# Attention ordered by pairs of heads, with sample attention in four rounds and the patterns combined in between

## Chip, cores and metric

One core of a Trainium2 chip runs the whole program. The time is the device time of one execution in microseconds (us). The engines work in parallel, each through its own queue in order, and meet at semaphores: TensorE (PE, with its weight loads PEld), VectorE (DVE), ScalarE (ACT), GpSimd (POOL) and SyncE (SP). SP and POOL issue the DMA transfers.

## The reference

One step of a decoder layer on a prompt of 2048 tokens and on 64 sample tokens (8 sequences of 8), 1024 channels wide. What matters here:

```python
proj = h @ w_in      # u, v, z of branch A; q, k, v of 3 patterns x 8 heads x 64; z of B; gates
DILATED_PAIRS = ((128, 1), (512, 4), (2048, 16))     # window, dilation
for gi, (window, dilation) in enumerate(DILATED_PAIRS):
    if kv_caches is None:   # prompt: causal band of window/dilation keys of the strided sequence
        acc, m, l = _dilated_prompt(q[:, :, gi], k[:, :, gi], v[:, :, gi], window, dilation)
    else:                   # sample: window/dilation + 1 keys out of the cache and the new rows
        acc, m, l = _dilated_sample(q[:, :, gi], k[:, :, gi], v[:, :, gi], kv_caches[gi], window, dilation)
...
wts = jnp.exp(ms - jnp.max(ms, axis=0))                    # over the three patterns, per head
attn = jnp.sum(wts[..., None] * accs, axis=0) / jnp.sum(wts * ls, axis=0)[..., None]
y_b = attn * silu(z_b)
```

So head slot j needs the results of all three patterns for slot j, and of no other slot. Branch A (gMLP gating), the merge of both branches and the output projection follow.

## The kernel before

All tensors are float32 outside; projections split each operand into two float16 halves and use three matmuls a product. The program runs in this order:

1. Conditioning and normalised inputs `hT`, with the first two projections of V mixed in.
2. The attention loop: 12 units `i` of a pattern `g` and a pair of heads `hp`, with `g, hp = divmod(i, 4)`: all four pairs of pattern 0, then of pattern 1, then of pattern 2. A unit has 8 steps. A step is `scores` (PE scores, masked minimum on DVE, exponentials on ACT, split into float16 halves `hl`, transposed by a DMA into `pT`) and, one step later, `values`. Between them, generators supply PE: `qk_proj(i + 1)` projects the next unit's queries and keys, and `extras(i)` the rest of V, the gate path `zb` and the gates. Results of a unit go to memory (`asc`).
3. `qk_proj` also transposes keys for the cache outputs (`kf` to `ko`, L746) right behind the projection's group, through the one PSUM bank `t`.
4. `sample_attention` is one generator, advanced two steps (`STEP1`) per step of the loop from unit 3 on. It computes key products of pattern 0, 1 and 2 for half the heads at a time (`ch` tiles of cache rows, product L472 and sum L473 on DVE) when `ready` says that all units of the pattern are projected, then a maximum over everything, then value products (L542, L547). Before each pattern, `repeat` copies the queries in memory 16 times (`qr`, 2 MB) and the new keys and values (`kr`); POOL issues these and all other transfers of the sample attention.
5. Branch A: projection of `v`, then gating. Between them `combine` weights the three patterns, one tile of 128 tokens and all heads at a time (16 calls), and the sample attention runs on. Its last step transposes `tot` (L573).
6. Merge and output projection.

The order that a reader sees is not the order that runs: a list scheduler places every engine's instructions by a simulated timeline, with the program's order as priority. It is fixed when the program is built.

Of the kernel before, what the change touches and what calls it, by code (L numbers as in the profile page):

```python
# [1 line left out]

# [16 lines left out]
SEQ = 2048  # L19
# [46 lines left out]
def body(ctx, tc, I, O):  # L66
# [18 lines left out]
    STEP1 = 2  # L85
# [31 lines left out]
    qr_d = [dram.tile([128, 8 * 512], F32, name=f"qr{g}") for g in range(3)]  # L117
    kr_d = [[dram.tile([NS, (8, 1)[g] * 512], F32, name=f"kr{g}{k}") for k in range(2)] for g in range(2)]
# [207 lines left out]
    def plan():  # L326
        qk = lambda i: [(o + i * 128, 128) for o in (OQ, OK)]
        order.extend((OVV + u * 256, 256) for u in range(2))
        order.extend(qk(0))
        for i in range(12):  # L330
            if i < 11:
                order.extend(qk(i + 1))
            if i < 4:
                order.append((OVV + 512 + i * 256, 256))
            elif i < 6:
                order.append((OZB + (i - 4) * 256, 256))
# [51 lines left out]
    def sample_attention(sp):  # L388
# [7 lines left out]
        tot = sp.tile([64, 2, 260], F32, name="tot")  # L396
        m_d = dram.tile([128, 64], F32, name="m_d")
        mn_d = dram.tile([64, 8], F32, name="mn_d")
        ma_d = dram.tile([64, 8], F32, name="ma_d")

        def repeat(g):
# [3 lines left out]
            for k, d in enumerate((ks_d, vs_d)):  # L405
                if g == 0:
                    GDMA(kr_d[0][k], bass.AP(tensor=d[0].tensor, offset=d[0].offset,
                                             ap=[[4096, 8], [0, 8], [1, 4096]]))
                elif g == 1:
                    GDMA(kr_d[1][k], bass.AP(tensor=d[1].tensor, offset=d[1].offset,  # L410
                                             ap=[[4096, 8], [0, 2], [1, 2048]]))
            yield

        def rows4(g, j, u, kv, hh):

            t = sp.tile([128, 4, 256], F32, tag="ch", bufs=CHB, name="ch")
            c = caches[g]
            pstep, r0 = ((8, j), (32, 4 * j), (128, 16 * j + 4 * u))[g]
            GDMA(t, bass.AP(tensor=c.tensor, offset=c.offset + r0 * 1024 + kv * 512 + hh * 256,  # L419
                            ap=[[pstep * 1024, 128], [1024, 4], [1, 256]]))  # L420
            return t

        def pairs(g, kv, hh):

            if g == 0:
                for j0 in (0, 4):
                    t = rows4(0, j0, 0, kv, hh)
                    for i in range(4):
                        for u in range(2):
                            yield t[:, i:i + 1, :].to_broadcast([128, 4, 256]), 4 * u, j0 + i, None  # L430
            elif g == 1:
                for j in range(8):
                    t = rows4(1, j, 0, kv, hh)
                    yield t, 0, j, None
                    yield t, 4, j, t
            else:
                for j in range(8):
                    for u in range(2):
                        t = rows4(2, j, u, kv, hh)
                        yield t, 4 * u, j, t  # L440

        def new_rows(g, n0, n, kv, hh):
            t = sp.tile([64, 4, 256], F32, tag="pr", bufs=1, name="nw")
            d = (ks_d, vs_d)[kv][g]
            c = slice(hh * 256, hh * 256 + 256)
            if g == 0:
                GDMA(t[:, 0:n, :], kr_d[0][kv].rearrange("p (n c) -> p n c", n=8)[:, n0:n0 + n, c])
            else:
                GDMA(t[:, 0, :], d[:, c])
                if g == 1:  # L450
                    GDMA(t[:, 1, :], kr_d[1][kv][:, c])
            return t[:, 0:n, :]

        NEW = [(0, 0, 0, 4), (0, 4, 4, 4), (1, 8, 0, 2), (2, 10, 0, 1)]

        Sx = [sp.tile([128, 8, 8, 8], F32, name=f"S{g}") for g in range(3)]
        Sn = sp.tile([64, 11, 8], F32, name="Sn")
        mp = sp.tile([128, 3, 8, 8], F32, name="mp")

        for g in range(3):  # L460
            for hh in range(2):
                cs = slice(hh * 256, hh * 256 + 256)
                h4 = slice(hh * 4, hh * 4 + 4)
                if hh == 0:
                    while ready[0] < g:
                        yield
                    yield from repeat(g)
                q = sp.tile([128, 8, 256], F32, tag="qa", bufs=1, name="q")
                GDMA(q, qr_d[g].rearrange("p (t c) -> p t c", t=8)[:, :, cs])
                for rows, t0, j, own in pairs(g, 0, hh):  # L470
                    dst = own if own is not None else sp.tile([128, 4, 256], F32, tag="pr", bufs=1, name="pr")
                    V.tensor_tensor(dst, rows, q[:, t0:t0 + 4, :], op=ALU.mult)  # L472
                    V.tensor_reduce(Sx[g][:, j, t0:t0 + 4, h4], dst.rearrange("p t (h c) -> p t h c", h=4),  # L473
                                    axis=AX.X, op=ALU.add)
                    yield
                qn = sp.tile([64, 1, 256], F32, tag="qn", bufs=1, name="qn")
                GDMA(qn[:, 0, :], qs_d[g][:, cs])
                for (gg, i0, n0, n) in NEW:
                    if gg == g:
                        k = new_rows(g, n0, n, 0, hh)  # L480
                        V.tensor_tensor(k, k, qn.to_broadcast([64, n, 256]), op=ALU.mult)
                        V.tensor_reduce(Sn[:, i0:i0 + n, h4], k.rearrange("p n (h c) -> p n h c", h=4), axis=AX.X,
                                        op=ALU.add)
                yield
            if g < 2:
                V.tensor_tensor(Sx[g], Sx[g], cms[:, g].unsqueeze(3).to_broadcast([128, 8, 8, 8]), op=ALU.add)
            V.tensor_reduce(mp[:, g], Sx[g].rearrange("p j t h -> p t h j"), axis=AX.X, op=ALU.min)
            yield
        V.tensor_tensor(Sn, Sn, mnew.unsqueeze(2).to_broadcast([64, 11, 8]), op=ALU.add)


        V.tensor_tensor(mp[:, 0], mp[:, 0], mp[:, 1], op=ALU.min)
        V.tensor_tensor(mp[:, 0], mp[:, 0], mp[:, 2], op=ALU.min)
        mn = sp.tile([64, 8], F32, name="mn")
        V.tensor_reduce(mn, Sn.rearrange("p n h -> p h n"), axis=AX.X, op=ALU.min)
        GDMA(m_d, mp[:, 0].rearrange("p t h -> p (t h)"))
        GDMA(mn_d, mn)
        mg = sp.tile([8, 17, 64], F32, tag="pr", bufs=1, name="mg")
        GDMA(mg[:, 0:16, :].rearrange("b p c -> b (p c)"), m_d.rearrange("(b p) c -> b (p c)", b=8))
        GDMA(mg[:, 16, :], mn_d.rearrange("(b t) h -> b (t h)", b=8))  # L500
        ma = sp.tile([8, 64], F32, name="ma")
        V.tensor_reduce(ma, mg.rearrange("b p c -> b c p"), axis=AX.X, op=ALU.min)
        GDMA(ma_d.rearrange("(b t) h -> b (t h)", b=8), ma)
        m64 = sp.tile([64, 8], F32, name="m64")
        GDMA(m64, ma_d)
        mb = sp.tile([128, 8, 8], F32, name="mb")
        pb = bank("t", bufs=TB)
        PE.matmul(pb[:, 0:64], selB, ma, start=True, stop=True)
        V.tensor_copy(mb, pb[:, 0:64].rearrange("p (t h) -> p t h", t=8))
        yield  # L510


        for g in range(3):
            V.tensor_tensor(Sx[g], Sx[g], mb.unsqueeze(1).to_broadcast([128, 8, 8, 8]), op=ALU.subtract)
            S.activation(Sx[g], Sx[g], AF.Exp, scale=-1.0)
            V.tensor_reduce(mp[:, g], Sx[g].rearrange("p j t h -> p t h j"), axis=AX.X, op=ALU.add)
            yield
        V.tensor_tensor(mp[:, 0], mp[:, 0], mp[:, 1], op=ALU.add)
        V.tensor_tensor(mp[:, 0], mp[:, 0], mp[:, 2], op=ALU.add)
        V.tensor_tensor(Sn, Sn, m64.unsqueeze(1).to_broadcast([64, 11, 8]), op=ALU.subtract)  # L520
        S.activation(Sn, Sn, AF.Exp, scale=-1.0)
        ln = sp.tile([64, 8], F32, name="ln")
# [719 lines left out]
```

## Time and profile before

| | |
|---|---|
| time, median of 3 runs | 2649.3 us (2641.63 to 2649.64) |
| the profiled execution | 2646.09 us; its span 2644.2 us |
| busy: PE, DVE, ACT, POOL | 2498.0, 1710.2, 981.4, 203.8 us |
| mean granted clock of PE | 0.974 |
| DMA | 392.24 MB, mean 148 GB/s; POOL's queue 73.71 MB of it |
| attention loop (first to last masked score) | 217 to 1447 us |
| branch A, then merge and output | from 1447 us; the last gating operation (L1100) starts at 2146.8 us |

How to read it: PE is busy nearly throughout, so what the other engines do matters where PE waits for them or where its granted clock falls below 1 behind a wait. A group's row gives busy time, mean duration in ns of one instruction, and idle time of its engine just before it with the releaser.

### The profile page before, as it was taken

To read this page: it belongs to the slowest core of one execution; us is meant where nothing else is said; L and a number is where in the kernel's file an instruction comes from. 1 tells how busy PE (TensorE), PEld (TensorE's weight loads), DVE (VectorE), ACT (ScalarE), POOL (GpSimd) and SP (SyncE) were. 2 spreads that over 40 slices of the span, in tenths; PEclk is the share of its full clock that TensorE was granted. 3 is DMA by queue.
4 is the path that set the end of the run, shared out by engine and by line. 5 is a ranking of instruction groups with operands and counts; after the bars stand their busy time and mean duration, and the time that the engine had idled before them with its cause. 6 is when DMAs were issued, how large, how long until landed. Compare 5 with 4: busy or idle time off the path is not lost.

```text
span 2644.2 us, 47549 instructions
## 1 busy us (share of the span) xinstructions
PE 2498.0 (94%) x18471; PEld 1777.3 (67%) x18471; DVE 1710.2 (65%) x3665; ACT 981.4 (37%) x2329; POOL 203.8 (8%) x223
## 2 busy tenths in 40 slices
PE   6999999899999899999998899999999699999998
PEld 3865776757767555555555678555555368898998
DVE  8655544888444787433478569899998535555653
ACT  7434544344555335445333222211111023443422
POOL 3000000000000010000021000100001101111110
PEclk8999999999999999999999999999999799999999
DMA  7233545556444577334577653665344237656552
GB/s 277 83 108 76 130 98 138 162 127 169 109 98 113 166 151 173 90 102 119 146 231 208 185 160 113 202 188 162 114 126 136 88 122 250 198 178 207 189 167 73
DMA packets 506673, 392.24 MB, mean 148 GB/s; under 512 B 180215, under 2 KB 443431, under 8 KB 505902
## 3 DMA queue, kind: packets, MB, share of 16 engines
q1 hardware_dynamic: 486718, 315.48, 42.6%
q0 software_dynamic: 19728, 73.71, 8.8%
q8 instruction: 145, 2.38, 0.4%
q14 instruction: 82, 0.67, 0.1%
HBM read 258.98 MB, written 99.43 MB: 136 GB/s over the span
## 4 chain that ended last, share of the span: by engine, by line
PE 51%; issue 19%; DVE 13%; DMA 12%; ACT 2%; POOL 1%; SPq 1%; DVEq 0%; POOLq 0%; ACTq 0%
PE mm L352 10%; PE mm L353 10%; PE mm L354 10%; DMA ch<-in_cache_kv_w 4%; PE mm L362 3%; PE mm L363 3%; PE mm L364 3%; PE s L828 2%; PE o L873 1%; DVE S L473 1%; DVE acc L547 1%; PE s L364 1%; PE s L362 1%; PE s L363 1%; POOL ch L419 1%
## 5 line engine op out<-in xcount | busy, mean ns | idle before, releaser
L352 PE MATMUL mm<-hH,hl 128*128 128x512 f16 (+2 forms) x2240 | 775.7, 346 | 10.2 <-DVE e L1099 4.5
L353 PE MATMUL mm<-hL,hl 128*128 128x512 f16 (+2 forms) x2240 | 774.6, 346 | 0.0
L354 PE MATMUL mm<-hH,hl 128*128 128x512 f16 (+2 forms) x2240 | 773.7, 346 | 0.0
L362 PE MATMUL mm<-hl,hH 128*128 128x256 f16 x1536 | 421.3, 276 | 7.5 <-ACT vt L625 2.8
L363 PE MATMUL mm<-hl,hL 128*128 128x256 f16 x1536 | 423.0, 276 | 0.8 <-DVE hL L617 0.7
L364 PE MATMUL mm<-hl,hH 128*128 128x256 f16 x1536 | 422.6, 276 | 0.4 <-DVE hl L308 0.4
L352 PEld LDWEIGHTS <-hl 128*128 128x128 f16 x2240 | 223.5, 100 | 185.0 <-issue 14.1
L353 PEld LDWEIGHTS <-hl 128*128 128x128 f16 x2240 | 221.6, 99 | 184.4 <-issue 17.4
L354 PEld LDWEIGHTS <-hl 128*128 128x128 f16 x2240 | 221.5, 99 | 183.9 <-issue 6.8
L838 ACT ACTIVATE p<-p,sg 128x256 f32<-128x256 f32 (+1 forms) x384 | 172.3, 451 | 177.9 <-DVE sg L836 152.4
L362 PEld LDWEIGHTS <-hH 128*128 128x128 f16 x1536 | 152.2, 99 | 30.3 <-issue 6.8
L363 PEld LDWEIGHTS <-hL 128*128 128x128 f16 x1536 | 152.0, 99 | 26.7 <-issue 6.3
L836 DVE CUSTOM_DVE_ANT_0 p<-s,masks,cqk 128x256 f32<-128x256 f32 (+1 forms) x384 | 140.5, 422 | 45.0 <-PE s L828 45.0
L296 DVE TENSOR_REDUCE mx<-wr 128x1 f32<-128x512 f32 x160 | 108.0, 681 | 93.5 <-DMA wr<-in_w_in 92.2
L364 PEld LDWEIGHTS <-hH 128*128 128x128 f16 x1536 | 152.1, 99 | 19.4 <-issue 0.7
L277 ACT ACTIVATE wh<-wr 128x512 fp32r<-128x512 f32 x160 | 99.8, 630 | 114.3 <-PE mm L353 71.0
L307 ACT ACTIVATE hl<-wr,scw 128x512 f16<-128x512 f32 x160 | 105.1, 712 | 98.1 <-DVE scw L303 95.6
L419 POOL DMA_DIRECT2D ch<-in_cache_kv_w x104 | 78.5, 755 | 816.0 <-DVE pr L542 241.5
L852 DVE SCALAR_TENSOR_TENSOR hl<-p,hl 128x1024 f16<-128x1024 f32 (+2 forms) x100 | 95.4, 954 | 69.5 <-ACT hl L851 68.6
L308 DVE SCALAR_TENSOR_TENSOR hl<-wr,scw,hl 128x512 f16<-128x512 f32 x160 | 113.4, 745 | 15.2 <-ACT hl L307 15.2
L1098 ACT ACTIVATE e<-mm,scw 128x512 f32<-128x512 f32 (+2 forms) x40 | 24.4, 611 | 250.8 <-PE mm L354 239.5
L352 PE MATMUL mm<-yaH,wh 128*128 128x512 f32 (+1 forms) x320 | 113.0, 353 | 1.9 <-DVE gts L1176 1.9
(445 smaller groups left out, 4384.5 us busy)
## 6 DMA issues: line engine op xcount, KB each, us to landing
ch<-in_cache_kv_w POOLq DMA_DIRECT2D x104, 512.0 KB, 4.6
wr<-in_w_in SPq DMA_DIRECT2D x160, 256.0 KB
wr<-in_w_proj_a SPq DMA_DIRECT2D x64, 256.0 KB
wr<-in_w_out SPq DMA_DIRECT2D x64, 256.0 KB
a<-sg SPq DMA_DIRECT2D x48, 264.0 KB
c<-a SPq DMA_DIRECT2D x48, 264.0 KB
v<-vt SPq DMA_DIRECT2D x96, 128.0 KB
vr<-v SPq DMA_DIRECT2D x48, 256.0 KB
```

The source lines that it names most:

```text
L296: V.tensor_reduce(mx[:, j:j + 1], raw.rearrange("p k c -> p (k c)"), axis=AX.X, op=ALU.max, apply_absolute_value=True)
L307: S.activation(HL[:, 0], raw, AF.Copy, scale=sc[:, 0:1])
L308: V.scalar_tensor_tensor(HL[:, 1], raw, sc[:, 0:1], HL[:, 0], op0=ALU.mult, op1=ALU.subtract)
L352: PE.matmul(pt, h, xh[:, t0:t0 + n], start=kc == 0, stop=False)
L353: PE.matmul(pt, h, xl[:, t0:t0 + n], start=False, stop=False)
L354: PE.matmul(pt, l, xh[:, t0:t0 + n], start=False, stop=kc == m - 1)
L362: PE.matmul(pt, xh[:, t0:t0 + n], h, start=kc == 0, stop=False)
L363: PE.matmul(pt, xl[:, t0:t0 + n], h, start=False, stop=False)
L364: PE.matmul(pt, xh[:, t0:t0 + n], l, start=False, stop=kc == m - 1)
L419: GDMA(t, bass.AP(tensor=c.tensor, offset=c.offset + r0 * 1024 + kv * 512 + hh * 256, ap=[[pstep * 1024, 128], [1024, 4], [1, 256]]))
L836: V.tensor_tensor_reduce(x, sb[e][:, j, 0:nk], masks[:, 256 - nk:256], scale=cqk[:, i:i + 1], scalar=3e38, op0=ALU.add, op1=ALU.min, accum ...
L838: S.activation(x, x, AF.Exp, bias=mc, scale=-1.0, accum_out=lc)
```

## The change

Units go by pair of heads: `g, hp = i % 3, i // 3`, so the three patterns of a pair follow one another. What depends on it moves with it:

- `plan`, `extras` and the first V projections follow the new order (V of heads 0 to 3 for the three patterns first, then `zb` and the second halves); `v_scale` works on one pattern and half the heads, and is called half a unit ahead of its use.
- `sample_attention` runs in four rounds, one per pair of heads, each with keys, maximum, values and output. It starts with the loop, three steps per step (`STEP1 = 3`); round `hp` may begin when unit `3 * hp + 1` is done. A `ch` tile holds 8 cache rows of 128 channels instead of 4 of 256. `repeat`, `qr_d` and `kr_d` are gone: eight transfers per pattern read the queries (and as many the new rows of patterns 0 and 1) straight into each group of partitions.
- `combine(hp, q)` takes one pair of heads and 512 tokens. Twelve of sixteen run inside the attention loop, in two parts with loads in the first; the others in the projection of `v`. None is left in the gating.
- PE's transposes of queries, keys and combined rows are put into a list, `later`; `flush(1)` runs all but the newest entry.

The core of the diff:

```diff
-    STEP1 = 2
+    STEP1 = 3
...
-            GDMA(qr_d[g], bass.AP(tensor=qs_d[g].tensor, offset=qs_d[g].offset,
-                                  ap=[[4096, 8], [0, 16], [1, 4096]]))
...
-                q = sp.tile([128, 8, 256], F32, tag="qa", bufs=1, name="q")
-                GDMA(q, qr_d[g].rearrange("p (t c) -> p t c", t=8)[:, :, cs])
...
+        for hp in range(4):
+            while ready[0] < hp:
+                yield
+            for (g, i0, n) in NEW:
+                q = sp.tile([128, 8, 128], F32, tag="qa", bufs=1, name="q")
+                for b in range(8):
+                    from_d(q[b * 16:b * 16 + 16], qs_d[g][b * 8:b * 8 + 8, :], hp, [[0, 16], [512, 8], [1, 128]])
...
+                for rows, t0, nt, j, own in pairs(g, 0, hp):
...
     def qk_proj(i):
-        g, hp = divmod(i, 4)
+        g, hp = divmod(i, 3)[::-1]
...
-                        p2 = bank("t", (128, 4, 128))
-                        for j, (a, w) in enumerate(parts):
-                            PE.transpose(p2[0:w, j, :], kf[:, a:a + w], ident)
...
+                        later.append(partial(key_rows, g, hp, t0, lo, parts, kf))
...
+    def flush(keep=0):
+        while len(later) > keep:
+            later.pop(0)()
...
-    def combine(i):
-        cc = cb.tile([128, 3, 528], F32, tag="c", bufs=1, name="c")
+    def combine(hp, q):
+        c = cb.tile([128, 3, 4, 132], F32, tag="c", bufs=1, name="c")
         for g in range(3):
-            DMA(cc[:, g, :], asc[g][i * 128:(i + 1) * 128, :])
+            DMA(c[:, g], rows_of(asc[g][:, hp * 132:(hp + 1) * 132], 0, q))
...
+        yield
...
-        pt = bank("s")
+        later.append(partial(y_rows, hp, q, zt))
...
+    sp = sx_.enter_context(tc.tile_pool(name="smp", bufs=1, side="right"))
+    smp[0] = sample_attention(sp)
     for i in range(12):
-        if i in (3, 7):
-            v_scale((i + 1) // 4)
-        if i == 3:
-            sp = sx_.enter_context(tc.tile_pool(name="smp", bufs=1, side="right"))
-            smp[0] = sample_attention(sp)
...
+        if i and i % 3 == 0:
+            todo_c = iter([x for q in range(4) for x in [combine(i // 3 - 1, q)] * 2])
         for b in range(8):
...
+            if b == 3 and i % 6 < 2:
+                v_scale(1 + i % 6, i // 6)
...
             for gen in todo[len(todo) * b // 8:len(todo) * (b + 1) // 8]:
                 next(gen)
+                flush(1)
...
             step(STEP1)
+            if i >= 3 and s % 3 == 0:
+                next(next(todo_c), None)
...
-        if i in (2, 6, 10):
-            ready[0] = (i - 2) // 4
+        if i % 3 == 1:
+            ready[0] = i // 3
```

What the scheduler makes of it, at three places. First POOL's queue at the start of the sample work (`qs`, `ks`, `vs` are the sample rows in memory, `qr`, `kr` their copies, `ch` a cache tile, `qn`, `nw` new rows). Before:

```order
L407 DMA kr_92<-vs_85 64x1x4096
L477 DMA qn<-qs_79 64x256
L410 DMA kr_94<-vs_86 16x1x2048
L403 DMA qr_88<-qs_79 128x1x4096
L469 DMA q<-qr_88 128x8x256
L407 DMA kr_91<-ks_82 64x1x4096
L419 DMA ch<-in_cache_kv_w 128x4x256
```

With the change:

```order
L406 DMA ch<-in_cache_kv_w 128x8x128 x2
L428 DMA q<-qs_79 16x8x128 x8
L458 DMA qn<-qs_79 64x128
L406 DMA ch<-in_cache_kv_w 128x8x128
L428 DMA nw<-ks_82 8x8x128 x8
L428 DMA q<-qs_80 16x8x128 x8
L458 DMA qn<-qs_80 64x128
```

The copies are gone; each load of `q` or `nw` is eight transfers, and the second pattern's `q` follows the first's at once.

Second, DVE's queue in unit 4 of the attention, behind the masks of its fifth step (the custom operation `ISA p,sg<-s`; `kl` is a key eviction, `hl` the split of the exponentials, `mx` and `scw` belong to weights). Before:

```order
L836 ISA sg 128x1
L852 SCALAR_TENSOR_TENSOR hl<-p,hl 128x1024
L728 SCALAR_TENSOR_TENSOR kl<-mm,kh 128x4x64
L651 SCALAR_TENSOR_TENSOR zb<-zb 128x256
L301 TENSOR_SCALAR scw<-t 128x1
L302 TENSOR_SCALAR scw<-hsc,scw 128x3
L651 SCALAR_TENSOR_TENSOR zb<-zb 128x256
L303 RECIPROCAL scw<-scw 128x1
```

With the change:

```order
L839 ISA sg 128x1
L529 TENSOR_TENSOR acc<-acc,ch 128x8x128
L295 TENSOR_REDUCE mx<-wr 128x1
L904 TENSOR_TENSOR den<-den,wl__10423 128x8
L524 TENSOR_TENSOR ch<-ch,S_2565 128x1024
L717 SCALAR_TENSOR_TENSOR kl<-mm,kh 128x16x16
L297 TENSOR_REDUCE mx<-mx 128x1
L905 TENSOR_SCALAR den<-den 128x8
L855 SCALAR_TENSOR_TENSOR hl<-p,hl 128x1024
L529 TENSOR_TENSOR acc<-acc,ch 128x8x128
L906 RECIPROCAL den<-den 128x8
```

Sample value products (`acc`, `ch`) and a combine (`den`) now stand between the masks and the splits.

Third, DVE's queue where the sample attention ends (`tot` is its last sum, `Sn` the weights of the new rows; `zs`, `e` are the gating's). Before, behind the last gating operation of the seventh channel group:

```order
L1100 SCALAR_TENSOR_TENSOR zs<-e,scw,zs 128x320
L560 TENSOR_TENSOR nw<-nw,Sn 64x1024
L563 TENSOR_TENSOR tot<-tot,nw 64x256 x4
L560 TENSOR_TENSOR nw<-nw,Sn 64x1024
L563 TENSOR_TENSOR tot<-tot,nw 64x256 x4
L560 TENSOR_TENSOR nw<-nw,Sn 64x512
L563 TENSOR_TENSOR tot<-tot,nw 64x256 x2
L560 TENSOR_TENSOR nw<-nw,Sn 64x256
L563 TENSOR_TENSOR tot<-tot,nw 64x256
L567 TENSOR_TENSOR tot<-tot 64x256
L570 TENSOR_TENSOR tot<-tot,zs 64x256
```

With the change, in the gating's third group of channels:

```order
L550 TENSOR_TENSOR nw<-nw,Sn 64x256
L553 TENSOR_TENSOR tot<-tot,nw 64x128 x2
L550 TENSOR_TENSOR nw<-nw,Sn 64x128
L553 TENSOR_TENSOR tot<-tot,nw 64x128
L1112 SCALAR_TENSOR_TENSOR e<-e,mm 128x512
L1079 SCALAR_TENSOR_TENSOR zs<-s_22326,lngb,Bt 128x512
L555 TENSOR_TENSOR tot<-tot 64x128
L1113 SCALAR_TENSOR_TENSOR zs<-e,scw,zs 128x512
L556 TENSOR_TENSOR tot<-tot,zs 64x128
L1106 SCALAR_TENSOR_TENSOR zs<-mm,scw,zs 128x512
```

Before, the sums stood alone at the end of the seventh of eight channel groups, with PE's transpose of `tot` behind that group's last matmul. Now they stand among the third group's operations, and PE's transpose stands inside a projection's matmuls.

More of the change, by code (lines that the diff above doesn't have):

```diff
@@ L1 @@
 from contextlib import ExitStack
+from functools import partial
 import numpy as np
@@ L326, in plan @@
     def plan():
-        qk = lambda i: [(o + i * 128, 128) for o in (OQ, OK)]
-        order.extend((OVV + u * 256, 256) for u in range(2))
+        qk = lambda i: [(o + (i % 3) * 512 + (i // 3) * 128, 128) for o in (OQ, OK)]
+        order.extend((OVV + g * 512, 256) for g in range(2))
         order.extend(qk(0))
@@ L436, in pairs, with from_d @@
             else:
                 for j in range(8):
[L438 to L443, printed above, removed]
+                    t = rows8(2, j, kv, hp)
+                    yield t, 0, 8, j, t
+        def from_d(t, src, hp, ap):
+            GDMA(t, bass.AP(tensor=src.tensor, offset=src.offset + hp * 128, ap=ap))
@@ L508, in sample_attention @@
[L508 to L516, printed above, removed]
-            yield
-        V.tensor_tensor(mp[:, 0], mp[:, 0], mp[:, 1], op=ALU.add)
@@ new lines, in sample_attention @@
+            t2 = th[:, 0:128].rearrange("p (h c) -> p h c", h=2)
+            V.tensor_tensor(t2, t2, th[:, 128:130].unsqueeze(2).to_broadcast([64, 2, 64]), op=ALU.mult)
+            V.tensor_tensor(th[:, 0:128], th[:, 0:128], z, op=ALU.mult)
+            for _ in range(4):
+                yield
+            pt = bank("t")
+            PE.transpose(pt[:, 0:64], th[:, 0:128], ident[0:64, 0:64])
+            yT = sp.tile([128, 64], F32, tag="yTs", bufs=1, name="yTs")
+            S.activation(yT, pt[:, 0:64], AF.Copy)
@@ new lines, in extras @@
+    def extras(i):
+        if i < 6:
+            return [((v_unit(2, 0), zb_unit(0), v_unit(0, 1), v_unit(1, 1), v_unit(2, 1), zb_unit(1))[i], 9)]
+        return [(gates(c), 5) for c in gate_units(i)]
+    v_scale(0, 0)
+    for _ in qk_proj(0):
+        flush(1)
+    v_load(0)
+    v_parts(0)
+    late = []
+    sp = sx_.enter_context(tc.tile_pool(name="smp", bufs=1, side="right"))
+    smp[0] = sample_attention(sp)
+    for i in range(12):
+        gens = ([(qk_proj(i + 1), 10)] if i < 11 else []) + extras(i)
+        todo = [gen for gen, k in gens for _ in range(k)]
+        if i and i % 3 == 0:
+            todo_c = iter([x for q in range(4) for x in [combine(i // 3 - 1, q)] * 2])
+        for b in range(8):
+            s = i * 8 + b
+            late.append(scores(s))
+            if b == 3 and i % 6 < 2:
+                v_scale(1 + i % 6, i // 6)
+            if b == 3 and i == 5:
+                v_scale(0, 1)
+            if s % 2 == 0 and s < 94:
+                v_load(s // 2 + 1)
+            for gen in todo[len(todo) * b // 8:len(todo) * (b + 1) // 8]:
+                next(gen)
+                flush(1)
+            if s % 2 and s < 95:
+                v_parts(s // 2 + 1)
+            if len(late) > LAG:
+                values(late.pop(0))
+            step(STEP1)
+            if i >= 3 and s % 3 == 0:
+                next(next(todo_c), None)
+        for gen, _ in gens:
+            for _ in gen:
+                assert False
+        if i % 3 == 1:
+            ready[0] = i // 3
@@ L966, in body @@
+    for state in late:
+        values(state)
+    flush()
+    ax.close()
+    sx = ExitStack()
+    ba = sx.enter_context(tc.tile_pool(name="ba", bufs=1))
     wT = ba.tile([128, 8, 128], F32, name="wT")
@@ L993, in spatial @@
         yield
-    left = iter(range(16))
+    left = iter([x for q in range(4) for x in [combine(3, q)] * 2])
     def combine_next():
-        i = next(left, None)
-        if i is not None:
-            combine(i)
+        flush()
+        for gen in left:
+            next(gen, None)
+            return
     def sides():
```

378 lines of the change are left out of this document (169 added, 209 removed).

## Prediction

> **What bounds the kernel now.** I read the busy time by stretches first, cut at the first masked score of every attention unit, then who TensorE (PE) waits for, and last the order of time around its longest waits.
>
> ```profile
> core 0: us, PE busy (x) PEld busy (x) DVE busy (x) ACT busy (x) POOL busy (x), PEclk, DMA share, GB/s
> 217.00:317.00 100.00, 100.00 (x915) 73.28 (x914) 49.96 (x140) 48.99 (x124) 0.55 (x1) 1.00 0.46 106
> 416.00:535.00 119.00, 109.10 (x966) 77.32 (x965) 84.00 (x173) 48.20 (x123) 3.50 (x5) 0.97 0.58 149
> 535.00:647.00 112.00, 104.74 (x946) 74.92 (x945) 97.46 (x187) 48.64 (x125) 6.24 (x9) 0.98 0.63 151
> 647.00:738.00 91.00, 90.43 (x871) 68.98 (x871) 46.80 (x133) 51.90 (x137) 0.54 (x1) 1.00 0.51 117
> 1157.00:1253.00 96.00, 96.00 (x699) 55.75 (x699) 37.06 (x124) 44.13 (x121) 0.00 (x0) 1.00 0.40 101
> 1253.00:1365.00 112.00, 105.18 (x738) 59.71 (x737) 68.54 (x153) 44.34 (x121) 14.14 (x20) 0.97 0.61 177
> 1365.00:1447.00 82.00, 70.86 (x516) 40.79 (x516) 63.38 (x125) 30.31 (x88) 13.63 (x18) 0.96 0.75 216
> ...
> 217.00:1447.00 1230.00, 1177.66 (x9731) 772.45 (x9730) 745.62 (x1758) 559.67 (x1459) 57.53 (x81) 0.98 0.55 138
> 1447.00:2644.00 1197.00, 1133.07 (x7430) 869.74 (x7428) 823.04 (x1566) 311.58 (x648) 113.65 (x119) 0.97 0.51 159
> ```
>
> (Stretch and its length, then each engine's busy time and number of instructions, PE's granted clock, share of the DMA engines.) TensorE bounds it. Quiet units (from 217 and 1157) run with PE full, its clock full and VectorE (DVE) at 50 or 37%. Units with sample work (from 416, 535, 1253 and 1365: units 2, 3, 10 and 11) take 112 to 119 us for about the same matmuls; in the last, which projects nothing, PE has fewer. Had units 0 to 7 taken 100 us, three 96, and the last 68 (a little under its 70.86 busy), the attention stretch would be 800 + 288 + 68 = 1156 us. It took 1230: 74 us are lost there, of which PE is idle for 1230 - 1177.7 = 52; the rest is slow clock and short waits.
>
> ```profile
> PE t L746 <- ACT kf L743: 24.9, 7, 8.1
> PE t L573 <- DVE tot L570: 22.6, 2, 20.7
> PE s L828 <- DVE sg L836: 7.9, 4, 3.2
> PE t L769 <- DVE vx L767: 5.6, 2, 4.0
> ```
>
> (PE's waits: us in all, times, longest.) Where L746's large waits are, at the start of sample work on a pattern, DVE had stood still twice, each time behind a transfer:
>
> ```profile
> 464.15 1.38 DVE L296 TENSOR_REDUCE mx<-wr 128x1 f32<-128x512 f32 x2 [6.04 <-DMA wr<-in_w_in]
> 470.99 1.23 DVE L472 TENSOR_TENSOR pr<-ch,q 128x1024 f32<-128x1024 f32 x1 [4.47 <-DMA q<-qr]
> ...
> 883.15 1.45 DVE L296 TENSOR_REDUCE mx<-wr 128x1 f32<-128x512 f32 x2 [7.84 <-DMA wr<-in_w_in]
> 889.55 1.23 DVE L472 TENSOR_TENSOR pr<-ch,q 128x1024 f32<-128x1024 f32 x1 [3.16 <-DMA q<-qr]
> ...
> 1298.24 1.45 DVE L296 TENSOR_REDUCE mx<-wr 128x1 f32<-128x512 f32 x2 [7.06 <-DMA wr<-in_w_in]
> 1305.41 2.36 DVE L472 TENSOR_TENSOR ch<-ch,q 128x1024 f32<-128x1024 f32 x2 [3.01 <-DMA q<-qr]
> ...
> 1381.84 1.22 DVE L472 TENSOR_TENSOR ch<-ch,q 128x1024 f32<-128x1024 f32 x1 [4.50 <-DMA q<-qr]
> 462.99 0.94 POOL L469 DMA_DIRECT2D q<-qr  x1 [12.62 <-DMA qr<-qs]
> ```
>
> (Start, length, instruction, idle time ahead of it and its cause.) The 2 MB copy `qr<-qs` occupies the transfers for some 13 us; weights come 6 to 8 us late, and `q` follows the copy. DVE works in order, so the key evictions queued behind these two are late, and PE with them.
>
> **The change, part by part.**
>
> *The end of the sample work* moves from the end of the gating's seventh channel group (of eight) into the third. What goes:
>
> ```profile
> 2055.00:2070.00 15.00, 11.69 (x68) 7.79 (x66) 12.09 (x16) 0.47 (x1) 2.25 (x3) 0.77 0.49 163
> ...
> 2076.00:2097.00 21.00, 0.33 (x3) 0.19 (x3) 10.19 (x20) 0.41 (x1) 2.21 (x4) 0.55 0.14 42
> 2097.00:2118.00 21.00, 20.13 (x80) 9.19 (x81) 7.70 (x18) 4.86 (x8) 0.74 (x1) 0.80 0.27 87
> ```
>
> 20.7 us of wait before `tot`; 21 x 0.20 = 4.2 of slow clock behind it; in 2055-2070, where DVE's sample products crowd the gating, 15 - 11.7 x 0.77 = 6; the first `tot` wait, 22.6 - 20.7 = 1.9. Together 33. The 48 combine transposes that leave for the attention take 5 along (a quiet unit issues 915 matmuls in 100 us, 0.11 each). Tail: **-38 us**. Bounds: -25 (the last wait and its clock alone) and -55 (most of the stretch's 1197 - 1133 = 64 idle us). Next late there is the split of the gate rows just after 1447, which now shares DVE with key products of the last round; that wait stays.
>
> *Repeats through memory* go (`qr`, `kr`); `q` comes instead as eight transfers of 64 KB for each pattern and pair of heads, and new rows of two patterns in the same way. POOL issues 399 transfers where it issued 162.
>
> ```profile
> L469 POOL DMA_DIRECT2D q<-qr x6: 892/924/939, 463.0 to 1372.5; - x6
> DMA to landing us min/median/max: 6.5/7.9/9.2
> ...
> L477 POOL DMA_DIRECT2D qn<-qs x6: 527/536/547, 250.0 to 1284.6; - x6
> DMA to landing us min/median/max: 2.0/2.3/15.4
> ```
>
> (Issue in ns; the line behind each is the time to landing.) 237 x 0.54 = 128 us more on an engine that is busy 14 of 112 us at most in the unit rows: nothing by itself, since no other work of POOL's lies in the attention. A load of `q` becomes 8 x 0.54 + 2.3 = 6.6 us against a median of 7.9, with no copy of 2 MB ahead of it. The Trainium skill speaks against this edit: "DMA: Bandwidth & Descriptors", section "Measured (HBM→SBUF, 128 partitions, SWDGE, issued from GpSimd)", asks for transfers of 1 MiB and gives 0.95 us for one of 64 KB, 6.15 for 1 MB. By that, as an estimate, eight small ones cost 1.5 us more, and twelve loads 17 us if all lay on the path, 2611 in the sum below; the landings above say otherwise, and I go by them.
>
> *Transposes put off* (`later`: a key transpose waits until the next entry comes) and V's scales computed half a unit ahead: the waits of L746 and L769, 30.5 of the 52 idle us. I give them the same share of the 74 lost: 43 go, 31 stay on six dense units, 5 each. If the cover fails (a transpose entered when its copy is late all the same), they come back one by one at 2 to 8 us.
>
> *DVE in the attention* pays for all this.
>
> ```profile
> 217.00:1455.00 1238.00, 117.10 (x96) 0.98 0.55 139
> ...
> L955 DVE TENSOR_TENSOR c<-c 128x512 f32<-128x512 f32 x16 | 10.9, 681 | 0.0
> ...
> L303 DVE RECIPROCAL scw<-scw 128x1 f32<-128x1 f32 x68 | 10.7, 158 | 0.9
> ```
>
> (DVE time of the key product L472, all inside the attention; a product of a combine; a small operation.) A second operation of that size goes with it, and as many pairs for the values lie all behind the attention, so sample work is 4 x 117 = 468 us, half of it in the attention; now three rounds of four are, and the start of the last: some +120 us. Of 16 combines 12 come in, each six operations of 0.68 and ten of 0.16: 12 x 5.7 = 68. I counted DVE's instructions from one unit's first mask to the next in both orders and priced them by their rows, less the 0.06 us by which neighbours overlap. Before, units 0 to 11 come to 48, 48, 83, 99, 46, 47, 80, 81, 36, 35, 68, 63; the rows say 50, 84, 97, 47, 37, 69 and 63 for those shown, so the count holds. After: **91, 66, 42, 81, 90, 74, 87, 105, 62, 94, 84, 53**, together 929. PE needs 96 to 100 in each but the last. Only unit 7 exceeds it (+5). Eight units are as dense as the six were: 8 x 5 = 40, +5, and 5 in the last: 50 us lost instead of 74. Transposes and small matmuls that come in add 7. Attention: 1156 + 50 + 7 = 1213, **-17 us**. A dense unit's loss is bounded by 0 (unit 3, with DVE busy 97 of 112 us, lost 12, but unit 4 won 9 back) and by 9 (unit 10 lost 16, its share of L746 some 7): attention -57 to +15.
>
> *Past other queues.* SP now issues a combine's four loads and its store among weight loads and the `pT` transposes, into one buffer; if the combine before it is late on DVE, all that stands behind them is late too. I price that within the 5 us, since SP waits for DVE's `hl` anyway. The DMA share, 0.46 in a quiet unit and 0.6 in a dense one, will be near 0.6 throughout. The new order of V's units and the smaller scales move work of equal size.
>
> **Sum.** Span 2644.2, 2646.1 with what lies around it: 2646 - 38 - 17 = 2591. The runs' median, 2649.3, is 3 above that execution: **2594 us**.
>
> **Rivals.**
> 1. *The denser DVE costs nothing.* For it: 1156 - 929 = 227 us of slack, and units 3 and 4. Against: units 10 and 11 lost 16 + 14 with DVE busy 61 and 77%. Attention 1168, time 2549.
> 2. *The gain is eaten.* Each dense unit loses 12 like unit 3 and no neighbour returns it: 8 x 7 = 56 more, 2650.
> 3. *Slower: the starts multiply.* The eight `q` transfers can start only when the pattern before has given up its one buffer, and DVE stands in order behind them. Three pattern starts cost up to 8 us of PE (L746) and 3 of clock (119 x 0.03) each. Now there are twelve; at 10.5 each that is 126, time 2720. It decides from 55 / 12 = 4.6 us per start. Against: 6 to 8 of those idle us came from the weights, late behind a copy that is gone; at 1381 DVE waited 4.5 us for `q` alone, and PE's longest wait for a mask is 3.2.
> 4. *The end does not move*: round four runs late through POOL's longer queue, and PE stands before `tot` as now. Tail -10, time 2622.
>
> **How the numbers follow.** About 0.3% (8 us) can be told from no change here. Forecast 0.60 (own range 2560 to 2628, faster); rival 1 0.12, faster; rival 4 0.05, faster; rival 2 0.13, of it 0.04 faster, 0.06 same, 0.03 slower; rival 3 0.10, of it 0.02 same, 0.08 slower. Faster 0.81, same 0.08, slower 0.11. Without the far half of rival 1, the slower part of rival 2 and rival 3: 2548 to 2652.
>
> **What would show it.** Right: weights no longer late behind a copy, the waits of L746's successor under 8 us in all, no PE gap over 5 us in the gating, DVE 75 to 85% busy in the attention, that stretch 1200 to 1230 us. Wrong: over 60 us of PE waits on `zt`, `tot` or masks there, DVE idle behind `q` or `nw` at twelve starts, a clock under 1 in most units.

## The result, and the profile after

The changed kernel takes 2675.9 us (median of 4 runs, 2673.6 to 2678.1), the kernel before 2645.5 beside it: a ratio of 1.0117, 95% interval 1.009 to 1.0144. It is about 30 us slower, where 52 less was forecast. Its profiled execution has a span of 2676.2 us.

The windows, cut as before at the first masked score of a unit (units 0, 2, 4, 7, 9 and 11, then the whole attention and the rest):

```profile
core 0: us, PE busy (x) PEld busy (x) DVE busy (x) ACT busy (x) POOL busy (x), PEclk, DMA share, GB/s
212.00:329.00 117.00, 110.49 (x949) 78.11 (x948) 91.51 (x201) 49.33 (x125) 18.50 (x31) 0.97 0.64 143
...
441.00:538.00 97.00, 94.29 (x848) 69.46 (x847) 45.15 (x153) 42.98 (x125) 3.22 (x6) 1.00 0.39 97
...
643.00:757.00 114.00, 106.23 (x944) 77.36 (x943) 89.47 (x201) 50.69 (x129) 14.07 (x19) 0.97 0.76 192
...
970.00:1102.00 132.00, 112.00 (x800) 63.55 (x798) 103.31 (x224) 49.02 (x122) 10.33 (x12) 0.92 0.68 155
...
1198.00:1320.00 122.00, 113.27 (x840) 65.06 (x839) 92.92 (x212) 47.62 (x119) 23.40 (x36) 0.96 0.72 164
...
1428.00:1515.00 87.00, 77.54 (x561) 46.58 (x562) 53.62 (x135) 32.15 (x92) 22.81 (x36) 0.90 0.72 185
212.00:1515.00 1303.00, 1208.63 (x9837) 793.92 (x9836) 936.58 (x2259) 568.01 (x1498) 190.16 (x300) 0.97 0.62 149
1515.00:2676.00 1161.00, 1113.48 (x7371) 859.28 (x7368) 658.00 (x1315) 303.09 (x625) 121.58 (x138) 0.99 0.45 137
```

The attention went from 1231 to 1304 us (+73; -17 forecast), the rest from 1196 to 1161 (-35.5; -38 forecast), the start is 5 shorter. PE is idle for 1303 - 1209 = 94 us of the attention, where it was 52. L746's waits of 24.9 us have no single successor among PE's waits in that stretch (us in all, times, longest):

```profile
PE mm L349 <- ACT gt L651: 13.1, 3, 9.5
PE s L831 <- DVE sg L839: 12.1, 8, 4.1
PE t L299 <- ACT ko L748: 11.9, 4, 3.8
PE t L772 <- DVE vx L770: 9.1, 3, 5.1
PE t L744 <- ACT ko L736: 6.8, 1, 6.8
```

The waits are spread: on evictions, on masks, and on the one PSUM bank `t` until ACT has copied an earlier key transpose (`ko`). The key transposes themselves, now L744, wait 13 us in all. Unit 7, the worst with 132 us, holds one place where all engines stand. In order of time (start, length, instruction, idle time ahead of it and its cause), POOL's issue of a cache load, then DVE around it, then ACT:

```profile
1043.98 0.88 POOL L406 DMA_DIRECT2D ch<-in_cache_kv_w  x1 [13.25 <-DVE w__14284 L907]
```
```profile
1048.01 0.68 DVE L913 TENSOR_TENSOR c<-c 128x512 f32<-128x512 f32 x1
1060.50 1.22 DVE L524 TENSOR_TENSOR ch<-ch,S 128x1024 f32<-128x1024 f32 x1 [11.80 <-DMA ch<-in_cache_kv_w]
```
```profile
1061.19 1.09 ACT L651 ACTIVATE gt<-mm,scw 128x512 f32<-128x512 f32 x2 [15.03 <-DMA gt<-gt]
```

The load issued at 1044 landed at 1060; DVE stood 11.8 us for it, ACT 15 us for the store of a gate, and PE 9.5 us behind ACT. The window of these 14 us:

```profile
1046.00:1060.00 14.00, 6.47 (x76) 5.05 (x74) 2.69 (x6) 0.16 (x1) 0.00 (x0) 0.80 0.97 104
```

The DMA share is 0.97 here at 104 GB/s, where the whole loop has 149 GB/s at 0.62: transfers were under way, and slow. The share adds up the times of packets and reads 1.23 in the 6 us from 1048, so it doesn't say that the engines were at their limit, and what made these packets long is not shown. In the tail the 20.7 us of wait before `tot` are gone; 8.0 stand once in the gating, before the matmuls that sum `acc`, and 200 us of the gating run with PE full:

```profile
PE t L538 <- DVE acc L529: 8.0, 1, 8.0
```

```profile
1927.00:2127.00 200.00, 200.00 (x1203) 120.86 (x1202) 87.08 (x196) 23.74 (x38) 0.00 (x0) 1.00 0.18 56
```

### The profile page after: what moved, and what is told of

The parts are those of the page before. It is cut to its first block, busy times and chain, and to the rows that moved or that the text cites. A ratio compares the mean times of both kernels' runs of the same rounds, so it can differ in the third digit from the quotient of the medians.

```text
span 2676.2 us, 48231 instructions
## 1 busy us (share of the span) xinstructions
PE 2508.4 (94%) x18518; PEld 1787.1 (67%) x18518; DVE 1734.1 (65%) x3915; ACT 980.3 (37%) x2343; POOL 344.3 (13%) x460
## 4 chain that ended last, share of the span: by engine, by line
PE 45%; issue 23%; DMA 15%; DVE 11%; ACT 2%; POOL 2%; SPq 1%; DVEq 0%; POOLq 0%; ACTq 0%
PE mm L349 9%; PE mm L350 9%; PE mm L351 9%; DMA ch<-in_cache_kv_w 4%; PE mm L359 3%; PE mm L360 3%; PE mm L361 3%; DMA wr<-in_w_in 2%; DMA c<-a 2%; DVE S L464 1%; PE s L361 1%; PE s L359 1%; PE s L360 1%; DMA pT<-hl 1%; DVE pr L463 1%
## 5 line engine op out<-in xcount | busy, mean ns | idle before, releaser
L359 PE MATMUL mm<-hl,hH 128*128 128x256 f16 x1536 | 421.9, 277 | 18.8 <-DVE xsm L380 7.8
L406 POOL DMA_DIRECT2D ch<-in_cache_kv_w x104 | 93.4, 898 | 988.4 <-DVE pr L524 282.5
L277 POOL TENSOR_TENSOR wl<-wr,wh 128x512 fp32r<-128x512 f32 x48 | 64.0, 1333 | 651.4 <-ACT wh L276 271.0
```

The lines of the kernel that those rows point to most:

```text
L359: PE.matmul(pt, xh[:, t0:t0 + n], h, start=kc == 0, stop=False)
```

## The experiments

Every time is a median of at least four runs, and every ratio is to the kernel before on the same chip, with its 95% interval. "Attention" is the stretch from first to last masked score in the profiled execution.

**1. The added work, one kind at a time.** Combines behind the loop:

```diff
-            if i >= 3 and s % 3 == 0:
-                next(next(todo_c), None)
...
-    left = iter([x for q in range(4) for x in [combine(3, q)] * 2])
+    left = iter([x for h in range(4) for q in range(4) for x in [combine(h, q)] * 2])
```

> The changed kernel with all sixteen combines issued behind the attention, in the projection of v (the scheduler still pulls three of them into the last unit); order of units, rounds of sample work and put-off transposes stay. The attention took 1304 us in the changed kernel, 141 above the 1163 that the matmuls need at full clock. Theory A (the combine's loads and its in-order steps on DVE stall the loop): attention 1235 to 1255, the stretch behind it 5 to 15 longer, time 2620 to 2640. Theory B (the rounds of sample work stall it): attention 1290 to 1304, time at or above 2670. Theory C (the transposes that are put off, with the buffer and the PSUM bank that they hold): attention unchanged. Theory D (any DVE work costs alike: 141 lost us over some 440 us of added work, 0.32 each): nine combines of 5.7 us, so 16 us less, attention 1288.

(The stretch behind the loop also takes a step of a combine twice as often.) Sample attention behind it (`step(STEP1)` removed from the loop, the generator made after it):

> The changed kernel with the sample attention started behind the attention loop, two steps where one was and six where three were (the scheduler still pulls about a tenth of it into the last units); combines stay in the loop. Read for the attention stretch alone, since the stretch behind it now carries four rounds. Theory A: attention 1280 to 1304. Theory B: 1200 to 1230. Theory C: unchanged. Theory D: 0.32 x 320 us of sample work gone = 102 less, 1202.

Both:

> The changed kernel with both combines and sample attention behind the loop: what is left in the attention is the new order of units, the put-off transposes and the scales of V computed early. Theories A, B and D: attention 1163 to 1190. Theory C: 30 to 60 us stay, 1200 to 1225. If A and B add up, the sum of what the two single runs win; if either alone wins as much as both, the stall needs both.

The attention in the three, and the rest in the first:

```profile
214.00:1475.00 1261.00, 1192.86 (x9742) 782.34 (x9743) 895.07 (x2112) 561.23 (x1478) 185.93 (x293) 0.97 0.58 142
1475.00:2679.00 1204.00, 1138.80 (x7466) 877.89 (x7464) 704.33 (x1463) 312.08 (x646) 125.56 (x146) 0.97 0.48 145
```
```profile
218.00:1420.00 1202.00, 1166.22 (x9746) 771.24 (x9744) 644.78 (x1829) 569.49 (x1489) 39.66 (x65) 1.00 0.51 128
```
```profile
213.00:1398.00 1185.00, 1158.13 (x9680) 764.43 (x9679) 597.17 (x1678) 563.87 (x1465) 39.65 (x65) 0.99 0.48 117
```

Without either, the attention takes 1185 us. The scheduler pulled 13 of the 104 cache loads, with their products, into the first two units, not the last; these take 117 us each. Those that it left free of sample work take 94 to 100, and the last, with fewer matmuls, 66: the new order of units costs nothing by itself, and theory C (1200 to 1225) fails. Combines alone add 17, sample work alone 76, both 119: 26 more than their sum. A mere change of order can move as much as the 17 and the 26 (experiment 5); the 76 is clear of that. So neither A nor B holds alone, and D meets the second run (1202) but not the first (1288 forecast, 1261). Behind the loop the combines cost 43 (1204 against 1161), as much as they cost in it beside the sample work (1304 against 1261): time 2680.8, ratio 1.0133 (1.011 to 1.0157). The other two, with all sample work in the tail, took 2934.2 (1.1093, 1.1067 to 1.1119) and 2982.5 (1.127, 1.1236 to 1.1304), and say nothing of the whole.

**2. Loads against DVE time.** One kernel keeps DVE's work and drops the cache loads (`t = one`, a resident tile, in `pairs`), the other keeps the loads and cuts the products to 8 of 128 channels (shown for the key products; their sums and the value products likewise):

```diff
-                    V.tensor_tensor(dst, rows, q[:, t0:t0 + nt, :], op=ALU.mult)
+                    V.tensor_tensor(dst[:, :, 0:8], rows[:, :, 0:8], q[:, t0:t0 + nt, 0:8], op=ALU.mult)
```

> The changed kernel without the loads of the cache: two tiles are loaded once, and all sample products read the first of them (pattern 2 writes into the second), so the sample results are left out; every DVE instruction keeps its size and place. With both kinds of work behind the loop the attention took 1185 us, with the sample work alone in it 1261, with both 1304: the sample work costs 76 to 102. Theory E (the loads are the price: DVE in order behind `ch` tiles that land late, 72 us of its waits, and cache packets that slow the DMA transposes): attention 1195 to 1245. Theory F (DVE's own time is the price: products of 0.7 to 1.2 us stand in order ahead of masks and evictions): attention 1280 to 1304.

> The changed kernel with all loads in place and the sample products cut to 8 of 128 channels (the rest is left out), so that each DVE instruction of 0.7 to 1.2 us becomes one of some 0.15 to 0.2, and some 250 us of DVE work leave the loop. Theory E: attention 1280 to 1304, or longer, since loads are asked for faster. Theory F: 1205 to 1235.

Attention without loads, then with small products:

```profile
214.00:1444.00 1230.00, 1187.20 (x9844) 785.05 (x9842) 936.26 (x2264) 569.97 (x1501) 120.34 (x222) 0.99 0.51 125
```
```profile
214.00:1519.00 1305.00, 1210.41 (x9842) 793.43 (x9840) 686.57 (x2260) 569.90 (x1499) 189.98 (x300) 0.97 0.62 149
```

These two runs decide between the theories. With DVE as busy as ever (936 us) but no loads: attention 1230, time 2582.1, ratio 0.976 (0.9736 to 0.9783). With 250 us of DVE work gone (687 us) but all loads: attention 1305, time 2672.7, ratio 1.0095 (1.0069 to 1.0121). Both lie in theory E's ranges and neither in F's; D (any DVE work costs alike) fails with F. The scheduler also reordered when the loads went: in the traces 594 of DVE's 3915 instructions have another place. The empty change of order in experiment 5 moved 681 and was worth 23 us, against 94 here.

Two ends stay open. In the kernel with small products DVE stood longer for cache tiles in the loop, 97 us instead of 57, so part of the time set free went into waiting for loads. And without loads the attention is still 67 us above the 1163 of the prediction's sum. No run leaves out both, so it isn't shown that DVE's work is free once the loads are gone.

Who stood for the loads, beside DVE, shows on ACT (in the changed kernel, then without loads):

```profile
ACT gt L651 <- DMA gt<-gt: 23.3, 5, 15.0
ACT hl L854 <- DMA pT<-hl: 18.8, 9, 4.7
ACT zb L636 <- DMA szb<-zb: 29.0, 9, 11.2
```
```profile
ACT gt L657 <- DMA gt<-gt: 8.7, 3, 3.6
ACT hl L860 <- DMA pT<-hl: 1.0, 2, 0.7
ACT zb L642 <- DMA szb<-zb: 26.5, 9, 6.4
```

The DMA transposes of the loop and the stores of `gt` land late when the cache loads run beside them; ACT's waits for the stores of `zb` hardly change.

**3. The size of a load's pieces.** The changed kernel reads 512 bytes of a cache row at a time, the one before 1 KB.

```diff
-            GDMA(t, bass.AP(..., offset=c.offset + r0 * 1024 + kv * 512 + hp * 128,
-                            ap=[[pstep * 1024, 128], [1024, 8], [1, 128]]))
+            GDMA(t.rearrange("p (n a) c -> p n (a c)", a=2),
+                 bass.AP(..., offset=c.offset + r0 * 1024 + kv * 512 + hp // 2 * 256,
+                         ap=[[pstep * 1024, 128], [1024, 4], [1, 256]]))
```

> The changed kernel with each cache load taking 4 rows of 256 channels instead of 8 rows of 128, as before the change: as many bytes and tiles, pieces of 1 KB in memory instead of 512 bytes; the products then read the wrong values (sample results left out). Without the loads the changed kernel took 2582 us, 94 less. Theory I (the halved pieces are what made the loads dear): 2625 to 2650, mean landing back from 6.2 to about 4.6 us. Theory J (bytes and the moment of the load count, not the pieces): 2668 to 2680.

Issue (ns, minimum, median and maximum) and landing of the 104 loads, in the changed kernel and with 1 KB:

```profile
L406 POOL DMA_DIRECT2D ch<-in_cache_kv_w x104: 882/889/975, 157.4 to 1871.4; - x104
...
DMA to landing us min/median/max: 4.2/6.2/16.5
```
```profile
L406 POOL DMA_DIRECT2D ch<-in_cache_kv_w x104: 748/752/848, 159.1 to 1845.1; - x104
...
DMA to landing us min/median/max: 4.0/5.4/9.6
```

2646.3 us, ratio 0.9997 (0.9976 to 1.0017): 30 us less for the same bytes. By the traces 73 of DVE's 3915 instructions have another place, and 4 of ACT's, far fewer than with the empty step of experiment 5. The time is in theory I's range, but the median landing came back to 5.4 us only, and the pieces are 30 of the 94 us that the loads cost, not the whole. The same edit without put-off transposes, and the opposite one in the kernel before:

> The changed kernel without put-off transposes (2639 us) and with cache loads in pieces of 1 KB (sample results left out). If both costs add up (30 for the pieces): 2605 to 2615. If the pieces hurt only together with put-off transposes (without them the loads cost 64 instead of 94): 2630 to 2640.

> The kernel before without copies (2624 us), with each cache load taking 8 rows of 128 channels instead of 4 of 256: as many bytes and tiles, pieces of 512 bytes as in the changed kernel (sample results left out). If the piece is what costs: in the changed kernel 104 loads became 30 us cheaper by 1 KB pieces (9 where no transpose was put off), so here 10 to 30 dearer, 2634 to 2655. If the pieces matter only where the loop holds rounds and combines: 2618 to 2630.

2630.2 (0.9946, 0.9926 to 0.9966), only 9 less than the 2639.4 of experiment 5; and 2644.5 (0.9985, 0.997 to 1.0), 21 more than the 2623.8 of experiment 4, though there 386 of DVE's 3665 instructions moved. The sign is the same three times, the size 9 to 30 us; 9 and 21 are within what a change of order can do by itself, so the size is not settled. Nor is the part of the put-off transposes: the first time is in the range for pieces that hurt only beside them, the second in that for pieces that hurt by themselves. The Trainium skill, "DMA: Bandwidth & Descriptors", section "Specifications", gives 512 bytes as enough for line rate; by that the halved pieces would cost nothing. These loads, which ran beside other traffic, landed later in pieces of 512 bytes in all three pairs (medians 6.2 against 5.4 us, 5.9 against 5.2, 5.5 against 4.8), and there the measurement differs from the page.

**4. The copies alone.** The kernel before, with `repeat` removed and queries and new rows loaded in eight transfers each:

> The kernel before with one part of the change: the copies `qr` and `kr` are gone, and queries and new rows come by eight transfers straight from the sample rows, in its own order of units and with its own two halves of heads. If the copies made the weights and `q` late (three times 6 to 8 us of DVE and as much of PE's wait for key transposes, 24.9 us in all): attention 1205 to 1218 instead of 1231, time 2620 to 2635. If that loss belongs to the density of the sample work and not to the copies: attention 1225 to 1235, time 2640 to 2650.

> The kernel before without the copies (2624 us), and without the loads of the cache (sample results left out). Theory I: with 1 KB pieces the loads cost less than in the changed kernel, 40 to 60 us instead of 94: 2564 to 2584. Theory J: as much per tile, some 94: 2530.

2623.8 us, ratio 0.9911 (0.9881 to 0.9942): this part of the change, with the order that the scheduler makes of it, is worth 22 us. Attention 1207 instead of 1231, and the wait of the key transposes, now L751, is shorter:

```profile
PE t L751 <- ACT kf L748: 15.6, 7, 2.7
```

DVE's 15 us of waits for `q` are gone. Its waits for weights are not: near the three places of the prediction it still stands, with no copy ahead:

```profile
463.22 0.69 DVE L296 TENSOR_REDUCE mx<-wr 128x1 f32<-128x512 f32 x1 [6.20 <-DMA wr<-in_w_in]
...
870.63 1.42 DVE L296 TENSOR_REDUCE mx<-wr 128x1 f32<-128x512 f32 x2 [6.02 <-DMA wr<-in_w_in]
...
1281.07 0.69 DVE L296 TENSOR_REDUCE mx<-wr 128x1 f32<-128x512 f32 x1 [4.93 <-DMA wr<-in_w_in]
```

Without cache loads it takes 2584.6 (0.977, 0.9737 to 0.9802), at the upper end of theory I's range. The attention with the loads, then without:

```profile
213.00:1420.00 1207.00, 1168.50 (x9674) 767.32 (x9672) 750.40 (x1772) 561.85 (x1464) 100.17 (x165) 0.98 0.56 136
```
```profile
212.00:1393.00 1181.00, 1160.47 (x9673) 764.89 (x9672) 751.24 (x1772) 562.21 (x1463) 60.53 (x113) 0.99 0.49 115
```

So the loads cost 39 us there and 94 in the changed kernel. Without loads the two kernels, 2584.6 and 2582.1, are equal within what these runs tell apart.

**5. The transposes put off.** `flush()` in place of `flush(1)`:

> The changed kernel with no transpose put off: each is issued as soon as its entry comes, so that no buffer of ev is held over and the one bank t is used earlier. Theory C: attention 30 to 60 us shorter, 1245 to 1275, time 2615 to 2645, and ACT's waits for the stores of zb and gt fall back from 29 + 23 to about 6 + 3. Theories A, B and D: the waits of key transposes for their copies come back (24.9 us in the kernel before), attention 1304 to 1335, time 2676 to 2705.

> The changed kernel, transposes put off as there, with four `ev` buffers instead of three (two small sample tiles share a buffer with others to make room). Theory G (a transpose that is put off holds one of three buffers, so ACT stands before `zb` and `gt` until a store lands: 29 + 23 us of waits): the loss of 36 us returns, time 2636 to 2655, waits for the stores of zb and gt below 20 together. Theory H (the loss is the single PSUM bank `t`, where put-off transposes meet other users, some 45 us of PE's waits): 2665 to 2680.

> The changed kernel without put-off transposes (2639 us) and without the loads of the cache (sample results left out). If the put-off transposes hurt by stores that the cache loads make late (theory G with E), they cost nothing once the loads are gone: 2575 to 2590, like the 2582 with both. If they hurt by themselves (theory H): 36 less, 2546.

2639.4 us without them, ratio 0.9979 (0.996 to 0.9997): 36 less, with an attention of 1283. The time is in theory C's range, the attention is not; the 2676 or more of theories A, B and D did not come. A fourth buffer gives 9 of the 36, 2666.5 (1.0071, 1.0044 to 1.0099). The waits for the stores of zb and gt fall from 29 + 23 to 4 + 7 as theory G said, but the time stays in theory H's range: 41 us less of ACT's waits were worth 9. Without loads the put-off transposes cost 7 (2575.3; 0.9741, 0.9715 to 0.9768), as G with E said. How much of 36 is only the scheduler's new order? An empty step ahead of each round changes nothing else:

```diff
             while ready[0] < hp:
                 yield
+            yield
```

> The changed kernel with one empty step ahead of each round of sample work: no instruction more or less, only another order from the scheduler. If put-off transposes have a cost of their own, 2665 to 2690 as before. If what was put down to them is scatter between orders, anything from 2640 to 2690.

> The same empty step ahead of each round in the kernel without put-off transposes (2639 us). If put-off transposes have a cost of their own: 2630 to 2650, some 25 to 45 below the kernel with the empty step alone. If it is scatter: within 15 of that kernel.

2652.8 (1.0028, 1.001 to 1.0047) and 2644.4 (0.9998, 0.998 to 1.0016). The empty step alone won 23 us in the changed kernel and lost 5 in the other, and the put-off transposes cost 8 between these two. So an effect of less than some 20 us, read from two kernels whose orders differ, isn't shown here; what the put-off transposes cost lies between 8 and 36, and what share is their own stays open. The last run is the kernel without put-off transposes with two steps of sample work instead of three:

> The changed kernel without put-off transposes (2639 us, attention 1283, rest 1150) and with two steps of sample work per loop step instead of three, so that about one round of four leaves the loop. Theory D (0.3 lost us for each us of added DVE work in the loop, 0.2 behind it): with some 100 us moved, attention 1253, rest 1170, time 2625 to 2640. If the loss is made at the starts of rounds or by the combines, the attention stays above 1270 and the time grows to 2645 to 2665.

2676.2 (1.0111, 1.009 to 1.0133): a third less sample work in each step, and 37 us slower than with three. The attention fell from 1283 to 1266 and the rest grew from 1150 to 1196. Theory D (1253 and 1170) fails here too. What else differs was not followed up.

**6. The end of the sample work.** In the kernel without copies PE waits 32.2 us for the last sum:

```profile
PE t L578 <- DVE tot L575: 32.2, 1, 32.2
```

Five steps per gating group should bring it forward; eight empty steps ahead of the last two transposes move these and little else:

```diff
             V.tensor_tensor(th[:, 0:256], th[:, 0:256], z, op=ALU.mult)
+            for _ in range(8 * hh):
+                yield
```

> The kernel before without copies (2624 us), with five steps of sample work per channel group of the gating instead of three, and four empty steps ahead of the last sums' matmuls and transposes as in the change: the last sum of the sample work then stands behind the 25th of 40 gating groups instead of the 35th. There PE waited 32 us for that sum, and its clock was 0.80 over 100 us. If that wait comes from the place at the end of the gating: 2590 to 2605. If denser products move it elsewhere: 2615 to 2630.

> The kernel before without copies (2624 us), with eight empty steps ahead of the last two transposes of the sample work, which moves them some 420 rows down PE's order, behind the 38th of 40 gating groups. If PE's wait of 32 us there, and its clock of 0.80 behind it, come from the place in the order: 2590 to 2610. If DVE is that late at the end wherever the transposes stand: 2618 to 2630.

The five steps: 2687.7, ratio 1.0164 (1.0134 to 1.0193), with the same attention and two long waits in the tail:

```profile
PE t L560 <- DVE acc L552: 46.0, 2, 45.2
PE t L582 <- DVE tot L577: 32.1, 1, 32.1
```

The scheduler placed PE's matmuls ten groups earlier, and the last transpose ran only 26 us earlier, at 2051 instead of 2078; PE stood for the difference. The empty steps: 2596.7, ratio 0.98 (0.9774 to 0.9827). Without copies, then with the empty steps, the windows around that transpose:

```profile
2030.00:2130.00 100.00, 63.86 (x333) 34.99 (x333) 38.27 (x69) 7.80 (x14) 16.32 (x29) 0.80 0.17 56
```
```profile
1990.00:2090.00 100.00, 91.54 (x506) 51.25 (x504) 63.86 (x94) 9.89 (x17) 23.17 (x38) 0.97 0.29 94
```

The transpose runs at 2084 us of the span, no earlier than before; PE no longer waits for it. Only 6 of PE's instructions and 34 of DVE's 3665 have another place. This version, the kernel before without copies and with two transposes moved, beats both kernels: 2% under the one, about 3% under the other.

## Why the prediction was wrong, point by point

- *The step that failed* is the price of a dense unit, and in it a term put at nothing: the cache loads. The prediction counted DVE's load per unit (929 us; 936.6 measured, so the count held) and charged 5 us for each unit as dense as before, 50 in all over 1163. Measured: 1304 - 1163 = 141. Of these, 74 went when the loads were left out. The prediction wrote down a DMA share near 0.6 and drew no cost from it, and it never counted cache tiles. Before, 51 of 104 are issued in the loop; now 78, each of halved pieces. Loads cost the attention 26 us for 52 tiles in the kernel without copies (1207 - 1181), 74 for 78 in the changed one, and 67 for 78 in the one without put-off transposes (1283 - 1216): 0.5, 0.95 and 0.86 each. The 26 is no more than a change of order can do; the other two are.
- *What the loads leave*, 1230 - 1163 = 67, is nearer the 50 that were priced. With combines and most of the sample work behind the loop 22 remain. How the rest divides among DVE's work, the combines with their own loads, and the small transposes stays open: 250 us of DVE work removed moved the attention by 1 us, but with all loads in place.
- *Why it looked like DVE*: the crowded units of the kernel before have both, a busy DVE and a DMA share near 0.6, in the same rows. One trace can't part them. Units 3 and 4, read there as slack of DVE, can't part them either.
- *The combines in the loop* were priced as DVE time and put within the 5 us. They add 17 alone and 43 beside the sample work, and their loads are among what DVE waits for. The prediction took only 5 out of the tail for them, their transposes; issued there, more tightly than before, the whole combines cost 43.
- *The copies*: the reading of the three places was half right. `q` came late behind the copy, and those 15 us of DVE's waits went with it. The weights came late mostly for another reason: without copies DVE still stands 6.2, 6.0 and 4.9 us for them near these places, 17 of the 21 us before, and up to 7.8 in the changed kernel. Together with put-off transposes the copies were to return 43 of 74 lost us. Alone they returned 24, about what a change of order can do, though the shorter wait of the key transposes speaks for them. Eight small transfers instead of one cost nothing visible: DVE waits nowhere in the attention for a late `q` ahead of a product. The opposing estimate of 17 us did not come. It was also summed wrongly: eight transfers of 64 KB carry half of the 1 MB that they were set against, and six loads became twelve, so the two figures that the prediction quotes give an estimate of 12 x 7.6 - 6 x 6.15 = 54.
- *Put-off transposes and early scales* were counted as gains. The first cost 8 to 36; the wait for `vx` rose from 5.6 to 9.1.
- *The tail* came out at -35.5 against -38, so close partly by luck, since the parts are others. That the last wait and its clock are worth 25 is supported: moving two transposes took away a wait of 32 us and won 27. With the 43 of the combines, more than 65 should have gone. What took the rest back was not settled. The loads of the last rounds take part in it: 25 us for 24 tiles there (1160.5 - 1135.2), as much as the tail's 50 tiles cost in the kernel without copies (1205.0 - 1180.3).
- *The rivals*: none had the mechanism. Starts did not multiply (no wait for `q`), the end did move. Rival 1, that a denser DVE costs nothing, is borne out only for the products beside the loads, and the loads came with them. The signs named as right did not come: the key transposes wait 13 us, one gap in the gating is 8.0, DVE is busy 72% of the attention, and that takes 1304 us. The signs named as wrong were partly seen: 0.90 to 0.98 of clock in most units, waits on `t` and masks; DVE idle behind `q` was not.

## What to carry to other kernels

Before work is moved into a stage that another engine bounds, count what it brings by kind: its bytes and pieces in memory beside its engine time. To part them, run one kernel with the transfers left out, one with the arithmetic cut down, and one with both. Where a scheduler sets the order, run an empty change of order first: here it moved the time by up to 23 us, so a smaller difference between two orders shows little by itself. And where PE stands for a late result, moving PE's instruction behind other work can win what hurrying the result cannot.

## What the runs showed of the hardware

- As many bytes in pieces of 512 bytes took POOL 889 ns to issue and 6.2 us to land, in pieces of 1 KB 752 ns and 5.4 us (medians of 104 loads of 512 KB). The programs with 512 bytes took 9, 21 and 30 us longer in three pairs, of which only the 30 is clear of what a change of order did.
- A load of 512 KB took from 4.2 to 16.5 us to land, in the same program; where it took longest, the DMA engines moved less than the loop's mean (104 against 149 GB/s) at a higher share (0.97 against 0.62).
- Cache loads cost a loop that PE bounds 67 and 74 us for 78 of them in two orders, 0.86 and 0.95 each, and 26 for 52 in a third, though no matmul reads their tiles. ACT's waits for DMA transposes fell from 18.8 to 1.0 us when they went.
